# Block operands of the up projection behind the mixer's last tile, adds of squares on GpSimd, and the first up pair's root in a chain of its own

## The chip, the cores and the metric

One core of one Trainium2 chip. The metric is the time of the whole program on the device in microseconds (us). Before the change it was 1103.57 us, the median of three runs (1101.72 to 1104.21). The engines are TensorE (PE in the profile, PEld its weight loads), VectorE (DVE), ScalarE (ACT), GpSimd (POOL) and SyncE (SP). A measurement of this kernel can hardly tell less than 0.2%, some 2.2 us, from no change.

## What is computed

The reference is one layer of a streaming encoder trunk, for a prompt of 512 tokens and a sample of 64, all in float32 with a model width of 1024:

```python
y, c_new, sa, sb = _mixer(_rmsnorm(x, p['norm_mix'][l]), ...)      # gated delta net and gated linear attention
x = x + y
x = x + _cross_attn(_rmsnorm(x, p['norm_mem'][l]), mem_k[l], mem_v[l], p['w_mq'][l], p['w_mo'][l])
f, f_new = _conv_ffn(_rmsnorm(x, p['norm_ffn'][l]), p['w_up'][l], ..., p['w_down'][l], ffn_prev[l])
x = x + f
...
return (_rmsnorm(x, p['norm_final']), ...)

def _rmsnorm(x, g):
    y = x * lax.rsqrt(jnp.mean(x * x, axis=-1, keepdims=True) + EPS)
    return y * g
```

`_conv_ffn` multiplies by `w_up` (1024 to 2 x 2816), runs a causal depthwise convolution of width 3, gates one half with the SiLU of the other and multiplies by `w_down`. `_cross_attn` has four heads of 256 that look into 256 memory tokens. What matters here are the three last norms (`norm_mem`, `norm_ffn` and `norm_final`, called n2, n3 and final below): each needs, for every token, the sum of the squares of x over all 1024 features.

## The kernel before

Both token sets run together as 576 columns, with the features on the partitions: x is eight tiles `x[0]` to `x[7]` of 128 x 576. An up operand has 580 columns, since each token set has two columns of padding. Each product of float32 is made of three products of half-length parts: an operand is split into a high part (`xh`, `ach`, `sh`, written by an ACT cast) and a low one (`xl`, `acl`, `sl`, the difference, written by DVE or POOL), and weights likewise (`w`, where the low part of many of them is finished by a DMA that accumulates in memory, issued from POOL's queue behind an ACT copy). Many products of two tiles by two go through a scheme of seven products on sums of blocks (P1, P2, P3, Q4 to Q7), whose operands are differences such as `tu` and `tw`, split again.

**Order of the work.** The kernel's text does not put instructions in the order in which they run. A class `Driver` records them with a model of each engine's time. The main generator yields PE work in its order. Side work (norms, operands, convolutions) lies in chains that `spawn` starts and that go on when what they have waited for is there: `yield [tiles]` waits for tiles, `yield WAIT` and `yield (key,)` for something in `drv.done`. Each instruction is put on its engine's queue by its modelled start, and `flush` (the line L257 of nearly all rows) issues it. `V`, `A` and `G` are DVE, ACT and POOL; `X` is whichever of DVE and POOL the model says ends sooner. A change in one chain can thus move rows of others.

**Squares.** `sq_acc` (L784) adds the square of one tile to a sum: ACT squares into `sq` (for the first tile into the sum itself), then X adds, `acc <- acc, sq`. It serves n2 (in `c_norm`, while the mixer's last product wo finishes its tiles), n3 (in `c_mo`, sum `facc`) and the final norm (in `last_tile`, in the tail). In the program before, all 19 of these adds went to DVE: 7, 7 and 5. `c_rstat` (L799) then reduces the sum over the partitions with one-column matmuls (`sm<-keep,acc`, ten in the trace for five token blocks), takes the root on POOL (`rt`), makes diagonal matrices `dg` on DVE and spreads them with matmuls (`sm<-dg,onesr`); ACT copies the outcome to `rbc`.

**Between the attention and the up projection.** The product mo of the attention's output adds into x. Tile 0 and tile 1 are plain products, the other six go through the scheme. PE does tile 0, then the three pairs, then tile 1 (`mo_last(1)`, read out of the large PSUM bank by `x<-big,x`). As soon as a tile of x is whole, `c_mo(m)` (L1879) squares it, scales it by the gain of n3 (`cx`), splits it to `xh` and `xl`, and marks `("mo", m)`. When both tiles of a pair are marked it spawns `c_sums(k)` (L1897), which makes the block operands of the up projection: `tu` and `tw` on DVE or POOL, their splits `sh`, `sl`, `sw`. They are used only from the fifth pair of up tiles on; the first four pairs (`JS = 4`) are plain. `first_up` (L1951) is the first up tile: it takes the x tiles in the order 2, 3, 4, 5, 0, 6 and then 7, 1, each as soon as it is marked.

**The first up pair.** An up pair is the tiles j and 22 + j, gate and value. Since the root of n3 is not there when the first pair ends, `raw_evac` copies that pair out of PSUM unscaled. The main loop then waited for "n3", called `use_norm("n3")` and spawned the convolution chains `c_gate` and `c_act` of pair 0, all ahead of the second pair's first tile. Later pairs are scaled by `rbc` when they are read out (`up_evac`).

**The tail.** The last stage is the down product; `last_tile` squares each finished tile of x into `acc` and scales it for the output (`gx`), and the last two tiles are done in halves with their own squares. One-column matmuls sum over the partitions, POOL makes the roots `rtf`, PE transposes, and `yo` rows scale the result.

PSUM has two large banks' tiles (`big`) and four small ones (`sm`): PE can start the next product in a bank only when the readout of the one before has been done.

Of the kernel before, what the change touches and what calls it, by code (L numbers as in the profile page):

```python
# [14 lines left out]
ALU = mybir.AluOpType  # L15
# [137 lines left out]
WAIT = "wait"  # L153
# [305 lines left out]
def tile_trunk(ctx, tc, xT, memT, wt, wd, vec, cst, w0, wgate, st_gdn, st_conv, st_gla, st_ffn, ckT, cv,  # L459
               o_y, o_gdn_p, o_conv, o_gla_p, o_ffn, o_mk, o_mv, o_gdn_s, o_gla_s):  # L460
    nc = tc.nc
    drv = PE = Driver(nc.tensor, nc.sync)
    V, A, G = Engine(drv, "V", nc.vector), Engine(drv, "A", nc.scalar), Engine(drv, "G", nc.gpsimd)
    X = Either(V, G)
# [19 lines left out]
    def slot(s="s", dt=F32, w=SLOT):  # L484
        return drv.rotate("s", NS, sp.tile([P, w], dt, tag="s", name=nm(s)))
# [42 lines left out]
    def r4(ap, b=128):  # L528
        return ap.rearrange("p (a b) -> p a b", b=b)
# [254 lines left out]
    def sq_acc(acc, x_, first, w=T):  # L784
        s = acc if first else slot("sq")
        A.activation(s[:, :w], x_[:, :w], AF.Square)
        if not first:
            X.tensor_tensor(acc[:, :w], acc[:, :w], s[:, :w], op=ALU.add)

    def ssq(accs, t, n, ps):  # L790

# [51 lines left out]
    def use_norm(key):  # L843
        N["rt"], N["rbc"] = N[key]
# [89 lines left out]
    def conv_raw(ps, copy):  # L934
        u = slot("u")
        for o, i in zip(two(u, 3, 518), pv(ps)):
            copy(o, i)
        return u
# [564 lines left out]
    def parts2(h, lo, src):  # L1503
        A.copy(h, src)
        X.tensor_tensor(lo, src, f(h), op=ALU.subtract)
# [8 lines left out]
    def hl2(src, new=None):  # L1514
        h, lo = [(new or slot)(s, F32R) for s in ("ach", "acl")]
        parts2(h[:, 0:T], lo[:, 0:T], src[:, 0:T])
        return h[:, 0:T], lo[:, 0:T]
# [66 lines left out]
    def main():  # L1584
        acc = slot("acc")
# [50 lines left out]
        for k in range(KT + 1):  # L1636
            for i, ps in enumerate(first2):
                j = k - i
# [31 lines left out]
        u0 = conv_raw(b0[0], A.copy)  # L1670
# [98 lines left out]
        def c_gate(g0, g1, r):  # L1769
            yield [g0, g1]  # L1770
            X.tensor_tensor(g1[:, N2], g1[:, N2], r[:, N2], op=ALU.mult)
            X.tensor_tensor(g0[:, 0:T], g0[:, 0:T], r[:, 0:T], op=ALU.mult)
            A.activation(g1[:, 0:T], g1[:, 0:T], AF.Tanh, scale=-0.5)
            A.activation(g0[:, 0:T], g0[:, 0:T], AF.Tanh, scale=0.5)
# [36 lines left out]
        acc = slot("acc")  # L1811
# [84 lines left out]

        def c_sums(k):  # L1897

            (eh, el, ce), (oh_, ol_, co) = fx[2 * k], fx[2 * k + 1]
            yield [ce, co]  # L1900
            u, w = slot("tu"), slot("tw")
            X.tensor_tensor(u[:, U1], ce[:, U1], ce[:, U2], op=ALU.subtract)
            X.tensor_tensor(u[:, U2], co[:, U2], ce[:, U2], op=ALU.subtract)
            yield [u]
            V.scalar_tensor_tensor(w[:, U1], u[:, U2], -1.0, ce[:, U1], op0=ALU.mult, op1=ALU.subtract)
            h, lo = slot("sh", F32R), slot("sl", F32R)
            parts2(h[:, 0:580], lo[:, 0:580], u[:, 0:580])
            yield [w]
            V.scalar_tensor_tensor(w[:, U2], w[:, U1], -1.0, co[:, U1], op0=ALU.mult, op1=ALU.subtract)
            w1 = slot("sw", F32R)  # L1910
            parts2(w1[:, U1], w1[:, U2], w[:, U1])
            sops[k].update({"P1": (eh[:, U1], el[:, U1]), "P2": (oh_[:, U1], ol_[:, U1]), "P3": (oh_[:, U2], ol_[:, U2]),
                            "Q5": (h[:, U1], lo[:, U1]), "Q7": (h[:, U2], lo[:, U2]), "Q6": (w1[:, U1], w1[:, U2]), "Q4": (eh[:, U2], el[:, U2])})
            drv.done.add(("sops", k))
            while not drv.ready("plain"):
                yield WAIT
            parts2(eh[:, U2], el[:, U2], w[:, U2])
            drv.done.add(("sop4", k))
# [51 lines left out]
        def states(col, u):  # L1970
            G.tensor_copy(u[:, 514:516], fst[:, col, :])
            G.tensor_copy(fout[:, col, :].rearrange("p (a b) -> p a b", b=2), pads(u))

        def up_tile():
            u = slot("fu")
            G.memset(u[:, 0:2], 0.0)
            return u

        def up_evac(col, ps):
            u = up_tile()  # L1980
            if isinstance(ps, Pair):
                V.together([("tensor_tensor", (u[:, 2 + c:292 + c], ps[:, i, 0:290], N["rbc"][:, c:c + 290]), dict(op=ALU.mult)) for i, c in ((0, 0), (1, 290))])
            else:
                V.tensor_tensor(r4(u[:, 2:582], 290), ps[:, :, 0:290], r4(N["rbc"][:, 0:580], 290), op=ALU.mult)
            states(col, u)
            return u
# [67 lines left out]
        def c_act(j, u, raw=False):  # L2054
            c1 = yield from up_conv(NJ + j, u, raw)
            while not drv.ready(("gate", j)):
                yield WAIT
            if j == NJ - 1:
                DMO(o_ffn, fout)
            c0 = cs[j]  # L2060
            yield [c0, c1]
            for a, b in ((0, 0), (TP, TP + 2)):
                n = TP if a == 0 else TS
                X.tensor_tensor(c1[:, a:a + n], c0[:, b:b + n], c1[:, b:b + n], op=ALU.mult)
            p = max(q for q in range(4) if PART0[q] <= j)
            odd_ = (j - PART0[p]) % 2
            yield [c1]
            full[j] = hl2(c1)
            cs[j] = c1
            if odd_ and p == 3:  # L2070
                yield from inner(j - 1, j, cs.pop(j - 1), cs.pop(j), True)
            drv.done.add(("act", j))

        full, ops = {}, {}

        def inner(ke, ko, ce, co, whole):
# [20 lines left out]
        acc = slot("acc")  # L2097
        gx = []
        for kd, i in FFN[:-1]:
            if kd == "up":  # L2100
                j = i
                ba_, bb_ = [], []
                if j == 0:
                    ba_.append(wide())
                    yield from first_up(ba_[0])
                    xs = [(fx[k][0][:, 0:580], fx[k][1][:, 0:580]) for k in range(8)]
                else:
                    yield from tile_proj("up", j, xs, ba_, None, 580, wide)
                if j == 0:
                    yield from tile_proj("up", NJ, xs, bb_, None, 580, wide)  # L2110
                    u0, u1 = raw_evac(ba_[0]), raw_evac(bb_[0])
                    yield ("n3",)
                    use_norm("n3")
                    drv.spawn(c_gate(j, u0, True), 1)
                    drv.spawn(c_act(j, u1, True), 1)
                    continue
                drv.spawn(c_gate(j, up_evac(j, ba_[0])), 1)
                if j > 0:
                    yield from tile_proj("up", NJ + j, xs, bb_, None, 580, wide)
                if j == JS - 1:  # L2120
                    drv.done.add("plain")
                drv.spawn(c_act(j, up_evac(NJ + j, bb_[0])), 1)
            elif kd == "upx":
                yield tuple(("sop4" if i[1] == "Q4" else "sops", k) for k in range(4))
                yield from up_product(*i)
            elif kd == "dn1":
                m, p = i
                yield tuple(("act", j) for j in PARTS[p])
                wh, wl = weight("dn", i)
                ps = wide()  # L2130
                yield from proj(ps, wh, wl, act_of(p), late=True)
                V.together([("tensor_tensor", (xx, xx, i_), dict(op=ALU.add)) for i_, xx in pieces(ps, x[m])])
                if m == 7:
                    for k in PARTK[p]:
                        del full[k]
            elif kd == "dns":
                ks = PARTS[i[0][0][1][1]]
                yield tuple(("act", j) for j in ks)
                yield from products(i, [ops[k] for k in ks[0::2]], dn_finish)
            else:  # L2140

                yield tuple(("act", j) for j in PARTS[3][:-1])
                halves = []
                for m in i:
                    ps = big()
                    wh, wl = weight("dn", (m, 3), m == i[0], m != i[0])
                    yield from proj(ps, wh, wl, [full[k] for k in PARTK[3][:-1]], True, False, late=True)
                    halves.append((ps, wh, wl))
                yield (("act", NJ - 1),)
                for m, (ps, wh, wl) in zip(i, halves):  # L2150
                    yield from proj(ps, wh, wl, [full[NJ - 1]], False, True, k0=len(PARTS[3]) - 1)
                    for xx, i_ in zip(two(x[m]), pv(ps)):
                        V.tensor_tensor(xx, xx, i_, op=ALU.add)
                    last_tile(m)
# [277 lines left out]
```

## Time and profile before

| | us |
|---|---|
| median of three runs | 1103.57 |
| the profiled execution | 1103.1 |
| its span, first to last instruction | 1101.2 |
| PE busy | 1084.6 |
| DVE busy | 745.0 |
| ACT busy | 702.8 |
| POOL busy | 313.5 |
| mean granted TensorE clock | 0.997 of full |

PE works in 98% of the span, so the other engines count where PE waits for them. Such waits are listed by who was waited for. A row of the timeline gives the start, the duration, the engine, the operation, the tile written, `<-`, the tiles read, and the shape; neighbours of one kind are drawn together as "x2", and the bracket at a row's end is the idle time ahead of it and what ended that. All names carry no numbers there, so `acc` stands for the sums of all norms.

### The profile page before, as it was taken

What the parts mean: (1) busy time and instruction counts of PE and PEld (TensorE: products, weight loads), DVE (VectorE), ACT (ScalarE), POOL (GpSimd) and SP (SyncE); (2) the same over time, 40 slices, a digit from 0 to 9 for tenths busy, and PEclk for the clock granted to TensorE, in tenths of its full rate; (3) what the DMA queues carried; (4) which work ended last, traced back from release to release, by engine and by line L of the source; (5) the groups of instructions that cost most, each with busy time, mean ns of one, the idle gap of its engine ahead of it and who ended that gap; (6) DMA issues with size and microseconds to landing.
All of it is one profiled execution on the core that took longest, in us unless ns stands there. A gap on an engine that the chain in (4) does not pass through costs nothing. (4 is left out here: it accounts for less than half of the span.)

```text
span 1101.2 us, 21348 instructions
## 1 busy us (share of the span) xinstructions
PE 1084.6 (98%) x8206; PEld 1045.5 (95%) x8206; DVE 745.0 (68%) x1464; ACT 702.8 (64%) x1383; POOL 313.5 (28%) x541
## 2 busy tenths in 40 slices
PE   9999999999999999999999999999999999999997
PEld 8999989998988999999999999999999999999996
DVE  5666854864655866887655768667876677577665
ACT  6766646563755568476655658768866676667644
POOL 1344215230422232022101223234332342333221
PEclk9999999999999999999999999999999999999999
DMA  9666433353445788789683629767886886888844
GB/s 306 142 160 142 98 78 96 61 122 97 137 100 144 176 169 184 277 237 207 165 229 61 189 46 204 182 134 163 175 198 150 184 198 158 191 179 182 171 83 111
DMA packets 66885, 173.04 MB, mean 157 GB/s; under 512 B 7776, under 2 KB 14048, under 8 KB 66784
## 3 DMA queue, kind: packets, MB, share of 16 engines
q0 software_dynamic: 30096, 72.89, 38.7%
q1 hardware_dynamic: 36400, 98.26, 27.3%
q8 instruction: 65, 1.06, 0.4%
q10 hardware_dynamic: 288, 0.52, 0.1%
q14 instruction: 36, 0.29, 0.1%
HBM read 158.67 MB, written 5.37 MB: 149 GB/s over the span
## 5 line engine op out<-in xcount | busy, mean ns | idle before, releaser
L257 PE MATMUL big<-xh,w 128*128 128x256 f32 (+2 forms) x1568 | 290.7, 302 | 1.2 <-ACT xh L257 1.0
L257 PEld LDWEIGHTS big<-xh,w 128*128 128x128 f32 x1568 | 234.2, 189 | 7.0 <-issue 1.5
L257 POOL DMA_DIRECT2D w<-wt x147 | 133.6, 915 | 372.6 <-ACT w L257 314.5
L257 ACT ACTIVATE w<-wr 128x512 fp32r<-128x512 f32 (+3 forms) x180 | 142.9, 795 | 56.1 <-PE sm L257 25.2
L257 ACT CAST w<-wr 128x512 fp32r<-128x512 f32 (+3 forms) x201 | 158.8, 792 | 25.7 <-PE big L257 9.8
L257 PE MATMUL big<-xl,w 128*128 128x256 f32 (+2 forms) x784 | 167.9, 295 | 0.5 <-DVE xl L257 0.5
L257 PE MATMUL sm<-xh,w 128*128 128x290 f32 (+1 forms) x768 | 162.4, 298 | 0.0
L257 PEld LDWEIGHTS big<-xl,w 128*128 128x128 f32 x784 | 130.9, 188 | 1.0 <-DVE xl L257 0.9
L257 PE MATMUL sm<-ach,w 128*128 128x288 f32 (+2 forms) x624 | 127.1, 296 | 4.3 <-DVE x L257 2.4
L257 PEld LDWEIGHTS sm<-xh,w 128*128 128x128 f32 x768 | 126.9, 190 | 0.0
L257 PE MATMUL big<-ach,w 128*128 128x256 f32 x624 | 111.3, 296 | 0.3 <-ACT ach L257 0.3
L257 PEld LDWEIGHTS sm<-ach,w 128*128 128x128 f32 x624 | 101.0, 188 | 5.7 <-ACT gx L257 1.5
L257 PE MATMUL sm<-xl,w 128*128 128x290 f32 (+1 forms) x384 | 103.5, 299 | 0.0
L257 ACT CAST w<-ws 128x512 fp32r<-128x512 f32 (+1 forms) x124 | 73.4, 601 | 40.6 <-DVE ws L257 20.3
L257 PEld LDWEIGHTS big<-ach,w 128*128 128x128 f32 x624 | 94.7, 188 | 0.6 <-ACT ach L257 0.5
L257 PE MATMUL sm<-acl,w 128*128 128x288 f32 (+2 forms) x312 | 83.8, 295 | 0.0
L257 DVE TENSOR_TENSOR w<-ws,w 128x512 fp32r<-128x512 f32 (+1 forms) x91 | 60.3, 672 | 25.2 <-ACT w L257 24.0
L257 DVE SCALAR_TENSOR_TENSOR fc<-fu,vec,fc 128x578 f32<-128x578 f32 x88 | 70.5, 816 | 9.4 <-ACT fc L257 9.3
L257 PEld LDWEIGHTS sm<-xl,w 128*128 128x128 f32 x384 | 72.1, 191 | 0.0
L257 PE MATMUL big<-acl,w 128*128 128x256 f32 (+1 forms) x312 | 67.1, 297 | 0.3 <-DVE acl L257 0.3
L257 PE MATMUL sm<-sh,w 128*128 128x290 f32 x288 | 60.9, 296 | 0.0
L257 PEld LDWEIGHTS sm<-acl,w 128*128 128x128 f32 x312 | 58.2, 188 | 0.0
(396 smaller groups left out, 2211.1 us busy)
## 6 DMA issues: line engine op xcount, KB each, us to landing
wr<-wt SPq DMA_DIRECT2D x134, 512.0 KB, 5.7
w<-wt POOLq DMA_DIRECT2D x60, 512.0 KB, 6.8
w<-wt POOLq DMA_DIRECT2D x87, 256.0 KB, 6.1
wr<-wd SPq DMA_DIRECT2D x24, 384.0 KB, 5.5
w<-wd POOLq DMA_DIRECT2D x24, 384.0 KB, 6.6
w<-ws POOLq DMA_DIRECT2D x29, 256.0 KB, 4.7
x<-xT SPq DMA_DIRECT2D x16, 288.0 KB, 5.8
mem<-memT SPq DMA_DIRECT2D x8, 256.0 KB, 5.0
```

The costliest lines, as they stand in the source:

```text
L257: fn(*args, **kw)
```

## The change

Three edits:

1. `c_sums` waits until all eight tiles are marked `("mo", m)` before it makes block operands of any pair.
2. The add in `sq_acc` is always POOL's (`G` in place of `X`), in all three norms.
3. A new chain `c_first_up` waits for "n3" and then does what the main loop did for the first pair. The main loop waits for "n3" only in the second pair, ahead of the readout of its first tile.

```diff
--- before.py
+++ after.py
@@ -785,7 +785,7 @@
         s = acc if first else slot("sq")
         A.activation(s[:, :w], x_[:, :w], AF.Square)
         if not first:
-            X.tensor_tensor(acc[:, :w], acc[:, :w], s[:, :w], op=ALU.add)
+            G.tensor_tensor(acc[:, :w], acc[:, :w], s[:, :w], op=ALU.add)
 
     def ssq(accs, t, n, ps):
 
@@ -1896,6 +1896,8 @@
 
         def c_sums(k):
 
+            while not drv.ready(*(("mo", m) for m in range(8))):
+                yield WAIT
             (eh, el, ce), (oh_, ol_, co) = fx[2 * k], fx[2 * k + 1]
             yield [ce, co]
             u, w = slot("tu"), slot("tw")
@@ -2071,6 +2073,13 @@
                 yield from inner(j - 1, j, cs.pop(j - 1), cs.pop(j), True)
             drv.done.add(("act", j))
 
+        def c_first_up(u0, u1):
+            while not drv.ready("n3"):
+                yield WAIT
+            use_norm("n3")
+            drv.spawn(c_gate(0, u0, True), 1)
+            drv.spawn(c_act(0, u1, True), 1)
+
         full, ops = {}, {}
 
         def inner(ke, ko, ce, co, whole):
@@ -2109,11 +2118,9 @@
                 if j == 0:
                     yield from tile_proj("up", NJ, xs, bb_, None, 580, wide)
                     u0, u1 = raw_evac(ba_[0]), raw_evac(bb_[0])
-                    yield ("n3",)
-                    use_norm("n3")
-                    drv.spawn(c_gate(j, u0, True), 1)
-                    drv.spawn(c_act(j, u1, True), 1)
+                    drv.spawn(c_first_up(u0, u1))
                     continue
+                yield ("n3",)
                 drv.spawn(c_gate(j, up_evac(j, ba_[0])), 1)
                 if j > 0:
                     yield from tile_proj("up", NJ + j, xs, bb_, None, 580, wide)
```

**DVE at the end of the mo products.** The names are those of above with a number for each buffer: x_5763, x_5764 and x_5758 are x[6], x[7] and x[1]; acc_7741 is the sum of n3. Before:

```order
L257 TENSOR_TENSOR x_5764<-x_5764,sm_8249 128x288
L257 TENSOR_TENSOR sw_8368<-tw_8248,sw_8368 128x290
L257 SCALAR_TENSOR_TENSOR tw_8404<-tu_8403,cx_8284 128x290
L257 TENSOR_TENSOR sl_8431<-tu_8403,sh_8430 128x580
L257 TENSOR_TENSOR acc_7741<-acc_7741,sq_8432 128x576
L257 SCALAR_TENSOR_TENSOR tw_8404<-tw_8404,cx_8344 128x290
L257 TENSOR_TENSOR xl_8434<-cx_8435,xh_8433 128x580
L257 TENSOR_TENSOR acc_7741<-acc_7741,sq_8445 128x576
L257 TENSOR_TENSOR x_5758<-big_7840,x_5758 128x512
L257 TENSOR_TENSOR x_5758<-big_7840,x_5758 128x64
L257 TENSOR_TENSOR xl_8447<-cx_8448,xh_8446 128x580
L257 TENSOR_TENSOR sw_8464<-tw_8404,sw_8464 128x290
```

And now, from the same readout of x[7] on:

```order
L257 TENSOR_TENSOR x_5764<-x_5764,sm_8244 128x288
L257 TENSOR_TENSOR x_5758<-big_7842,x_5758 128x512
L257 TENSOR_TENSOR x_5758<-big_7842,x_5758 128x64
L257 TENSOR_TENSOR xl_8419<-cx_8420,xh_8418 128x580
L257 TENSOR_TENSOR xl_8431<-cx_8432,xh_8430 128x580
L257 TENSOR_TENSOR xl_8459<-cx_8460,xh_8458 128x580
L257 TENSOR_TENSOR tu_8461<-cx_8184,cx_8113 128x290
L257 TENSOR_TENSOR tu_8463<-cx_8251 128x290
L257 TENSOR_TENSOR tu_8463<-cx_8335,cx_8251 128x290
L257 TENSOR_TENSOR tu_8478<-cx_8420 128x290
```

The adds to the sum and the block operands' rows (`sw`, `sl`, `tw`) have left the stretch ahead of x[1]'s readout (`x_5758<-big`), which now follows the readout of x[7] directly. The block operands' `tu` rows stand behind the three `xl` rows.

**POOL at the same place.** The last adds to n3's sum, between the issues of the weights' DMAs, as they are now:

```order
L257 DMA w_8306<-wt 128x1024
L257 MEMSET cx_8460 128x2x2
L257 DMA w_8355<-wt 128x1024
L257 TENSOR_TENSOR acc_7744<-acc_7744,sq_8417 128x576
L257 TENSOR_TENSOR acc_7744<-acc_7744,sq_8429 128x576
L257 MEMSET rin_8540 128x8
L257 TENSOR_TENSOR acc_7744<-acc_7744,sq_8457 128x576
L257 DMA w_8553<-wt 128x1024
L257 MEMSET fu_8625 128x2
L257 MEMSET fu_8626 128x2
L257 TENSOR_TENSOR rt_8528<-rin_8540,mhalf 128x5
L257 DMA w_8556<-wt 128x1024
```

Before, POOL had here three `tu` rows and a `sw` row of the block operands, and no adds.

**DVE in the tail.** x_5761 and x_5762 are x[4] and x[5], acc_8449 and acc_8433 the final sum. Before:

```order
L257 TENSOR_TENSOR w_13223<-wr_13222,w_13223 128x512
L257 TENSOR_TENSOR x_5760<-x_5760,sm_13146 128x288
L257 TENSOR_TENSOR acc_8449<-acc_8449,sq_13251 128x576
L257 TENSOR_TENSOR acc_8449<-acc_8449,sq_13253 128x576
L257 TENSOR_TENSOR x_5761<-x_5761,sm_13212 128x288
L257 TENSOR_TENSOR x_5761<-x_5761,sm_13224 128x288
L257 TENSOR_TENSOR x_5762<-x_5762,sm_13212 128x288
L257 TENSOR_TENSOR x_5761<-x_5761,sm_13313 128x288
L257 TENSOR_TENSOR x_5762<-x_5762,sm_13212 128x288
L257 TENSOR_TENSOR acc_8449<-acc_8449,sq_13329 128x576
```

And now:

```order
L257 TENSOR_TENSOR w_13223<-wr_13222,w_13223 128x512
L257 TENSOR_TENSOR x_5760<-x_5760,sm_13146 128x288
L257 TENSOR_TENSOR x_5761<-x_5761,sm_13212 128x288
L257 TENSOR_TENSOR x_5761<-x_5761,sm_13224 128x288
L257 TENSOR_TENSOR x_5762<-x_5762,sm_13212 128x288
L257 TENSOR_TENSOR x_5761<-x_5761,sm_13292 128x288
L257 TENSOR_TENSOR x_5762<-x_5762,sm_13212 128x288
```

The three adds of 128 x 576 have left this queue; the readouts follow one another.

**PE at the last attention head.** `sm<-kvh,qh`, `kvl,qh` and `kvh,ql` are the scores of the last head, where the number of the second `qh` (before 7739, now 7742) is that of the head's last query tile; `big<-ach,w` and `big<-acl,w` are mo's first plain product. Before:

```order
L257 MATMUL sm_7721<-pth_7553,kvh_6733 128x512
L257 MATMUL sm_7721<-ptl_7554,kvh_6733 128x512
L257 MATMUL sm_7721<-pth_7553,kvl_6734 128x512
L257 MATMUL sm_7722<-pst_7559,cvr_7116 128x64
L257 MATMUL sm_7744<-kvh_7501,qh_7618 128x256
L257 MATMUL sm_7744<-kvl_7502,qh_7618 128x256
L257 MATMUL sm_7744<-kvh_7501,ql_7619 128x256
L257 MATMUL sm_7744<-kvh_7501,qh_7739 128x256
L257 MATMUL sm_7744<-kvl_7502,qh_7739 128x256
```

And now:

```order
L257 MATMUL big_7753<-ach_7236,w_7431 128x256
L257 MATMUL big_7753<-ach_7236,w_7431 128x320
L257 MATMUL big_7753<-acl_7237,w_7431 128x256
L257 MATMUL big_7753<-acl_7237,w_7431 128x320
L257 MATMUL big_7753<-ach_7236,w_7432 128x256
L257 MATMUL big_7753<-ach_7236,w_7432 128x320
L257 MATMUL sm_7789<-kvh_7505,qh_7621 128x256
L257 MATMUL sm_7789<-kvl_7506,qh_7621 128x256
L257 MATMUL sm_7789<-kvh_7505,ql_7622 128x256
L257 MATMUL sm_7789<-kvh_7505,qh_7742 128x256
L257 MATMUL sm_7789<-kvl_7506,qh_7742 128x256
L257 MATMUL sm_7789<-kvh_7505,ql_7743 128x256
```

Twelve mo matmuls, of which the last six are shown, now stand ahead of the scores. Before, the scores followed the preceding head's products with the values directly. Further on, n3's `sm<-dg,onesr` stand some 40 matmuls further down, in the first tile of the second up pair in place of the second tile of the first; behind that PE's order is as it was.

## The prediction

> **What bounds the kernel now.** I read the page first, then the waits of TensorE, then the chain of waits, and last the timeline around the three gaps that the change can reach.
>
> ```profile
> span 1101.2 us, 21348 instructions
> PE 1084.6 (98%) x8206; PEld 1045.5 (95%) x8206; DVE 745.0 (68%) x1464; ACT 702.8 (64%) x1383; POOL 313.5 (28%) x541
> ```
>
> PE (TensorE) is busy for 1084.6 of 1101.2 us. The change leaves every matmul in the program, so only the 16.6 us in which PE does not work, and stretches in which it works slowly, can be won. The profiled execution took 1103.1 us, 1.9 more than its span; it lies 0.47 under the median of the runs shown (1103.57, from 1101.72 to 1104.21).
>
> ```profile
> PE sm L257 <- DVE x L257: 2.4, 3, 1.3
> PE big L257 <- ACT xh L257: 1.0, 1, 1.0
> PE sm L257 <- ACT qh L257: 0.8, 1, 0.8
> PE big L257 <- DVE xl L257: 0.5, 2, 0.3
> PE sm L257 <- DVE ql L257: 0.3, 1, 0.3
> ```
>
> These rows give us in total, times, longest. The `xh` and `xl` waits stand between the attention's output products (tile family `mo`) and the up projection; one `x` wait of 1.3 stands in the tail; `qh` and `ql` stand ahead of the last head's scores. The other waits I leave as they are.
>
> **The gap between mo and up.** The timeline, with start, duration, engine and tiles:
>
> ```profile
> 683.68 1.04 ACT L257 CAST w<-wr 128x1024 fp32r<-128x1024 f32 x1
> ...
> 685.53 0.68 ACT L257 ACTIVATE sq<-x 128x576 f32<-128x576 f32 x1
> ...
> 686.37 0.43 PE L257 MATMUL big<-ach,w 128*128 128x256 f32 x2
> ...
> 687.03 0.75 DVE L257 TENSOR_TENSOR acc<-acc,sq 128x576 f32<-128x576 f32 x1
> ...
> 687.74 0.68 ACT L257 ACTIVATE sq<-x 128x576 f32<-128x576 f32 x1
> ...
> 689.92 0.81 DVE L257 TENSOR_TENSOR x<-big,x 128x512 f32<-128x512 f32 x2
> ...
> 690.82 0.69 ACT L257 ACTIVATE sq<-x 128x576 f32<-128x576 f32 x1 [0.46 <-DVE x L257]
> ...
> 692.44 0.68 ACT L257 CAST xh<-cx 128x580 fp32r<-128x580 f32 x1
> ...
> ...
> 693.17 0.54 PE L257 MATMUL big<-xh,w 128*128 128x290 f32 x2 [0.97 <-ACT xh L257]
> ...
> 693.96 0.54 PE L257 MATMUL big<-xl,w 128*128 128x290 f32 x2 [0.26 <-DVE xl L257]
> ...
> 694.34 1.16 PE L257 MATMUL sm<-keep,acc 128*128 128x1 f32 x10
> ```
>
> PE ended tile 1's product at 686.80, but DVE read it out only at 689.92, behind sums of squares and rows of the block operands, and ACT worked on operand casts meanwhile. So `xh` of tile 1 came at 693.12, and PE, free at 692.20 (693.17 less 0.97), waited 0.97 and then 0.26 for `xl`.
>
> In the changed order the readout follows the last readout of tile 7 directly and starts at about 686.9. ACT then sets the pace. With no operand casts, its square of tile 6 starts when the weight cast ends, 683.68 + 1.04 = 684.72. From square to square a tile takes 687.74 - 685.53 = 2.21, so tile 7 starts at 686.93 and tile 1 at 689.14. From tile 1's square to its `xh` are 692.44 - 690.82 = 1.62: `xh` runs 690.76 to 691.44, and `xl` follows to 692.20. PE wants `xh` at 692.20 and `xl` about 0.27 later. **Both waits go: 0.97 + 0.26 = 1.23 us**, with margins of 0.76 and 0.27.
>
> **The slow stretch behind it.** The windows (PE busy, ..., then the granted clock):
>
> ```profile
> 693.10:695.50 2.40, 2.08 (x15) 1.81 (x15) 2.40 (x5) 2.40 (x5) 1.14 (x1) 1.00 0.00 0
> 695.97:699.38 3.41, 3.41 (x16) 3.41 (x16) 2.28 (x9) 3.41 (x4) 3.17 (x4) 0.50 0.62 159
> 1086.40:1087.80 1.40, 1.40 (x15) 1.33 (x13) 1.13 (x5) 0.79 (x3) 0.00 (x0) 1.00 0.00 0
> ```
>
> Right behind these waits the clock stood at 0.50 for 3.41 us, in which PE does half of its work: 1.71 us lost. What preceded it is two gaps and ten one-column matmuls of 1.16 us in all. The tail's one-column matmuls at 1086.4, without a gap among them, kept 1.00, and the 1.33 gap at 1079.01, without such matmuls, is followed by no drop either (the mean clock of the run, 0.997, has room only for this stretch and one after PE's last work). So I take both to be needed, and without the gaps **1.71 us come back**. Bounds: 0, if the ten matmuls suffice, and 1.71.
>
> [...]
>
> **The squares on GpSimd.** No `acc` add ran on POOL before. The nearest row of its size, and the row of the adds on DVE:
>
> ```profile
> L257 POOL TENSOR_TENSOR acl<-ao,ach 128x576 fp32r<-128x576 f32 x2 | 2.8, 1424 | 21.6 <-ACT ach L257 21.6
> ...
> L257 DVE TENSOR_TENSOR acc<-acc,sq 128x576 f32<-128x576 f32 x26 | 19.6, 753 | 0.7
> ```
>
> So 19 adds leave DVE (19 x 0.753 = 14.3 us of its time, mostly in PE's shadow) and cost POOL 1.42 each, or 1.75 as in the row of 375.03 below, which has company on DVE; I take 1.42 where nothing collides. For `norm_ffn` the last three adds follow the squares that end at 685.4, 687.6 and 689.8: they end at 686.9, 689.1 and 691.3 (with 1.75, 691.6). PE reaches the ten matmuls that read the sum at about 692.20 + 2 x 0.27 = 692.75. Margin 1.2 us, so no wait. POOL's DMA for the next weights stands behind the last add, but it waits for ACT's cast of about 691.4 to 692.5 anyway.
>
> Where both engines run at once:
>
> ```profile
> 375.03 1.75 POOL L257 TENSOR_TENSOR acl<-tu,ach 128x576 fp32r<-128x576 f32 x1
> 375.10 2.30 DVE L257 TENSOR_TENSOR gt<-gt,gt 128x576 f32<-128x576 f32 x1
> ```
>
> A DVE row with two operands in SBUF, which alone takes 0.75 (the `acc` row has its shape), took 2.30: 1.55 longer. Each of the 19 adds can do this to a DVE row that makes an operand or stands ahead of a readout. In the two product stages (wo and mo, 7 adds each) DVE has rows of both sorts, but it is idle about a third of the time (68% busy), and PE has four banks of the small sort to go on with, so I expect few that reach PE. **I book 0.6 us of new waits; the bounds are 0 and, if all 14 of these adds passed on 1.55 less the 0.75 that each saves, 11 us.** [...]
>
> **The tail.**
>
> ```profile
> 1076.88 1.61 DVE L257 TENSOR_TENSOR acc<-acc,sq 128x576 f32<-128x576 f32 x2
> ...
> 1078.41 1.01 DVE L257 TENSOR_TENSOR x<-x,sm 128x288 f32<-128x288 f32 x2
> 1079.01 0.37 PE L257 MATMUL sm<-ach,w 128*128 128x288 f32 x1 [1.33 <-DVE x L257]
> ...
> 1082.63 0.67 ACT L257 ACTIVATE sq<-x 128x576 f32<-128x576 f32 x1
> ...
> 1085.41 0.48 DVE L257 TENSOR_TENSOR acc<-acc,sq 128x320 f32<-128x320 f32 x1
> ...
> 1086.48 0.28 PE L257 MATMUL sm<-keep,acc 128*128 128x1 f32 x2
> ```
>
> Two adds stood on DVE ahead of the readout that frees PE's bank. Without them it starts at about 1077.0 and ends at 1077.45, before PE wants the bank (1079.01 - 1.33 = 1077.68). **The gap goes: 1.33 us**, and all behind it moves up. POOL's last add then follows a square that ends at 1083.30 - 1.33 = 1081.97; the one before it ends at 1082.15, so the last ends at 1083.6 (with 1.75 each, 1084.2). DVE wants it for the add of 320 columns at 1085.41 - 1.33 = 1084.08. It just fits (or is 0.1 late), and PE wants the sum only at 1085.15. Bounds: 0 (POOL sets the end) and 1.33.
>
> **The order in the attention.** The moved n2 rows also shift the planner's choices: 12 mo matmuls now stand ahead of the last head's scores.
>
> ```profile
> 627.72 0.39 PE L257 MATMUL sm<-kvh,qh 128*128 128x256 f32 x1 [0.79 <-ACT qh L257]
> ...
> 632.22 0.28 PE L257 MATMUL sm<-kvh,ql 128*64 128x256 f32 x1
> ...
> 632.87 0.70 PE L257 MATMUL big<-ach,w 128*128 128x256 f32 x4
> ...
> 635.96 0.35 DVE L257 TENSOR_SCALAR e<-e,sc 64x256 f32<-64x256 f32 x1
> ```
>
> Four such matmuls took 0.70 and two (686.37, above) 0.43, so one more is 0.135. The twelve, 1.6 us, cover the 0.79 and the 0.3 for `ql`; `ach` is now cast ahead of `qh`, which costs 0.7 of that cover, so about 0.3 of the waits stays. **0.8 us gained**; bounds 0 and 1.09. The softmax behind the scores keeps 36 mo matmuls (4.9 us) as cover; from the last scores (632.50) to the last `e` (636.31) it took 3.8.
>
> **The first up pair's root.** Its `sm<-dg,onesr` matmuls go some 40 matmuls down, and with them the normalised readouts and convolutions of pair 0. The second pair's readout waits for the same root:
>
> ```profile
> 703.50 0.95 PE L257 MATMUL sm<-dg,onesr 128*128 128x512 f32 x4
> ...
> 711.67 0.76 DVE L257 TENSOR_TENSOR fu<-big,rbc 128x580 f32<-128x580 f32 x1 [0.88 <-PE big L257]
> ...
> 745.41 0.30 PE L257 MATMUL sm<-sh,w 128*128 128x290 f32 x1
> ```
>
> The readout begins when PE ends the tile. With the root's matmuls 40 x 0.135 = 5.4 later, at about 709, their 0.95 us and the copies of `rbc` behind them (some 0.7, as other ACT rows of 512 and more columns here) end near 710.6, so this costs PE nothing; a bank freed a us late is asked for again only a whole up tile later. The block operands are now made after 691.4; PE first reads them at 745.41, 54 us later. Nothing.
>
> **The sum.** 1.23 + 1.71 + 1.33 + 0.8 - 0.6 = 4.5 us: 1103.1 - 4.5 = 1098.6 by the profiled execution, 1099.1 by the median. I say 1099.0.
>
> **The rivals.**
>
> *The gate falls all the same* (0.20). The ten matmuls suffice, or some other short wait joins them: 4.5 - 1.71 = 2.8 us, 1100.3 to 1100.8. For it: they are there still. Against it: the tail's like stretch.
>
> *Late weights* (0.14). Adds wait for their squares with DMA issues behind them on POOL, and PE waits for weights as it did in this row:
>
> ```profile
> 664.72 0.93 PE L257 MATMUL sm<-ach,w 128*128 128x288 f32 x5 [0.93 <-DMA w<-wt]
> ```
>
> Two or three issues late by 1.42 cost 2.8 to 4.3 and take the gain back: 1101.5 to 1103. Against it: the adds stand between issues that wait for ACT casts for us on end.
>
> *The held port* (0.13), on the other side. In the wo and mo products the adds hold up DVE's weight sums and `xl` rows, the readouts queue behind them, and PE waits for banks. Each that reaches PE costs 1.55 - 0.75 = 0.8. It decides from (4.5 + 2.2) / 0.8, some 8 of the 14 adds: 1106 and more.
>
> *It does not do what it says*: POOL's chain of adds becomes the tail's end, 1.33 less gain, 1100. This lies in the forecast's range.
>
> **How the numbers follow.** The forecast, 1097 to 1101, has 0.53; with the three rivals that is 1.00. The low end of 1097.0 is the whole sum without new waits (5.1) and some 1 us of bank and weight waits in the mo products that may move; the high end of 1103.8 takes in late weights. Left out: the held port and some slivers. A measurement here can tell about 0.2%, 2.2 us, from no change: faster is under 1101.4. Faster 0.66 (0.50 of the forecast, 0.15 of the first rival, 0.01 of the second), same 0.20 (0.03, 0.05, 0.12), slower 0.14 (0.01 of late weights, and the port).
>
> **What would show it.** Right: no PE wait on `xh` and `xl` near 692; no clock of 0.5 before PE's last work; no 1.33 wait in the tail; `acc` rows on POOL of about 1.42; `sm<-keep,acc` near 691 with no wait ahead. Wrong: PE waits on POOL's `acc`; DVE rows of 2 us beside POOL's adds with PE waiting on `x`; longer waits on `w<-wt`.

## The result, and the profile after

The changed kernel takes **1098.71 us**, median of ten runs (1098.12 to 1101.05), against 1104.12 (1101.09 to 1106.91, ten runs) before: a ratio of **0.9954**, 95% interval 0.994 to 0.9968, so 5.1 us less by the ratio. The profiled execution took 1098.48 us. In a second comparison (experiment e10) the ratio was 0.9964 (0.9948 to 0.9979). The forecast was 1099.0, and the sum made against the profiled execution 1098.6.

The head of the page and the waits of PE (in total, times, longest) in the changed kernel:

```profile
span 1096.7 us, 21365 instructions
PE 1082.6 (99%) x8206; PEld 1043.8 (95%) x8206; DVE 736.6 (67%) x1449; ACT 703.5 (64%) x1383; POOL 342.7 (31%) x556
```

```profile
PE sm L257 <- ACT fu L257: 1.2, 2, 0.9
...
PE sm L257 <- DVE x L257: 0.8, 2, 0.6
PE sm L257 <- DMA w<-wt: 0.8, 1, 0.8
...
PE big L257 <- ACT w L257: 0.6, 1, 0.6
PE big L257 <- ACT ach L257: 0.5, 1, 0.5
PE sm L257 <- ACT w L257: 0.4, 1, 0.4
...
PE sm L257 <- DVE ql L257: 0.3, 1, 0.3
...
PE big L257 <- DVE xl L257: 0.2, 1, 0.2
```

Of the `fu` row, the kernel before had:

```profile
PE sm L257 <- ACT fu L257: 0.7, 1, 0.7
```

PE is busy for 2.0 us less with the same 8206 matmuls, which shows that it worked faster somewhere, and the span is 4.5 shorter. The `xh` and `qh` rows of before are gone, the `x` row has lost its wait of 1.3, and a second wait on `fu` and two on `w` are new. The `w` wait of 0.6 stands at 6.39, far ahead of the change's places; e1 and e11 have one of 0.8 there as well.

Between mo and up the timeline now reads:

```profile
685.30 0.82 DVE L257 TENSOR_TENSOR x<-big,x 128x512 f32<-128x512 f32 x2 [1.14 <-PE big L257]
...
685.63 1.44 POOL L257 TENSOR_TENSOR acc<-acc,sq 128x576 f32<-128x576 f32 x1 [0.76 <-ACT sq L257]
...
686.04 2.32 DVE L257 TENSOR_TENSOR xl<-cx,xh 128x580 fp32r<-128x580 f32 x2
...
687.84 1.81 POOL L257 TENSOR_TENSOR acc<-acc,sq 128x576 f32<-128x576 f32 x1 [0.73 <-ACT sq L257]
...
688.63 0.68 ACT L257 CAST xh<-cx 128x580 fp32r<-128x580 f32 x1
...
689.35 0.92 DVE L257 TENSOR_TENSOR xl<-cx,xh 128x580 fp32r<-128x580 f32 x1 [0.99 <-ACT xh L257]
...
690.65 0.43 PE L257 MATMUL big<-xh,w 128*128 128x290 f32 x2
...
691.20 0.28 PE L257 MATMUL sm<-keep,acc 128*128 128x1 f32 x2
```

The readout of tile 1 now waits for PE (1.14), not PE for it. `xh` ends at 689.31, and PE takes it up at 690.65 without a wait, and `xl` ends at 690.27. The last add on POOL ends at 689.65, 1.55 us ahead of the one-column matmuls. The clock, by windows (the granted clock stands behind POOL's column):

```profile
680.00:692.40 12.40, 12.40 (x95) 12.24 (x94) 8.52 (x16) 11.44 (x19) 6.86 (x10) 1.00 0.76 176
692.40:700.00 7.60, 7.60 (x57) 7.60 (x58) 5.80 (x16) 7.40 (x13) 5.25 (x4) 1.00 0.90 245
```

The 0.50 is gone and PE has no idle time in 20 us.

**Where the time came from.** Of single matmuls that are the same in both profiles, the starts:

| matmul | before | after | gained so far |
|---|---|---|---|
| `big<-xh,w`, ahead of the last head | 621.41 | 621.32 | 0.09 |
| `big<-ach,w`, behind its scores | 633.68 | 632.48 | 1.20 |
| `big<-xh,w`, first up tile | 691.50 | 690.11 | 1.39 |
| `big<-xh,w`, second up pair | 711.48 | 706.87 | 4.61 |
| `sm<-ach,w`, ahead of the tail's gap | 1077.39 | 1074.42 | 2.97 |
| `sm<-ach,w`, behind it | 1079.01 | 1074.57 | 4.44 |
| the last one | 1094.60 | 1090.06 | 4.54 |

The attention brought 1.1, the passage from mo to up 3.2, the tail 1.5; between the second up pair and the tail 1.6 were given back.

### The profile page after: what moved, and what is told of

It is laid out like the page before. It is cut to its first block, busy times and chain, and to the rows that moved or that the text cites. A ratio compares the mean times of both kernels' runs of the same rounds, so it can differ in the third digit from the quotient of the medians.

```text
span 1096.7 us, 21365 instructions
## 1 busy us (share of the span) xinstructions
PE 1082.6 (99%) x8206; PEld 1043.8 (95%) x8206; DVE 736.6 (67%) x1449; ACT 703.5 (64%) x1383; POOL 342.7 (31%) x556
## 4 chain that ended last, share of the span: by engine, by line
PE 90%; DMA 3%; ACT 2%; issue 2%; DVE 2%; POOL 1%; SPq 0%; DVEq 0%; ACTq 0%; POOLq 0%
PE sm L257 45%; PE big L257 45%; DMA w<-ws 2%; ACT w L257 1%; DMA w<-wt 1%; DVE ws L257 0%; DMA wr<-wt 0%; DVE fc L257 0%; POOL w L257 0%; ACT ach L257 0%; POOL ws L257 0%; ACT vraw L257 0%; DVE x L257 0%; DVE acl L257 0%; ACT fc L257 0%
```

## The experiments

Twelve kernels ran, in three groups of four, each group on one chip with runs of the kernel before: e1 to e4 and e9 to e12 on one chip, e5 to e8 on another. Ratios are against that kernel in the same group. The changed kernel itself did not run beside e5 to e8, so where these are set against it, its two ratios (0.9954 and 0.9964) are used. For the clock I count executions with a mean of 0.997 or less; of the kernel before, 52 of the 90 beside these experiments were such, and in the first group their median was 2.1 us above that of the others (1104.07 and 1101.93).

**e1, the first edit alone**

```diff
         def c_sums(k):
 
+            while not drv.ready(*(("mo", m) for m in range(8))):
+                yield WAIT
```

> The kernel before with the first edit alone: block operands wait for all eight tiles; adds stay where they were, the root stays in the main loop. My theory: what delayed tile 1 between mo and up was the work on block operands (DVE rows and ACT casts), and one add of 0.75 ahead of the readout can be borne, since x[7]'s readout ends at 685.7 and the readout could start at 686.85. So both waits (1.23) and the slow stretch (1.71) go: 2.9 to 3.2 us faster than before, the tail's wait of 1.3 and the attention's 1.1 stay. Rival: it was the adds on DVE that delayed tile 1; then the waits stay for the larger part and the gain is under 1 us.

Measured: 0.9983 (0.9973 to 0.9992), 1.9 us faster. Of this kernel:

```profile
686.37 0.82 DVE L257 TENSOR_TENSOR x<-big,x 128x512 f32<-128x512 f32 x2
...
689.69 0.68 ACT L257 CAST xh<-cx 128x580 fp32r<-128x580 f32 x1
...
691.27 0.75 DVE L257 TENSOR_TENSOR xl<-cx,xh 128x580 fp32r<-128x580 f32 x1
```

The readout came 3.5 us earlier than before, PE's wait on `xh` was gone, that on `xl` 0.07, and the clock stayed at 1.00: this edit alone clears the passage, and the adds on DVE were not its cause. The gain is smaller than the 2.9 to 3.2 expected. The slow stretch is not in each execution of the kernel before: 3 of 12 executions had the low clock here, 18 of 33 there, so what goes with it is an estimated 0.3 x 2.1 = 0.6 us in the median, not 1.71; with the 1.23 that makes the 1.9.

**e2, the second edit alone**

```diff
-            X.tensor_tensor(acc[:, :w], acc[:, :w], s[:, :w], op=ALU.add)
+            G.tensor_tensor(acc[:, :w], acc[:, :w], s[:, :w], op=ALU.add)
```

> The kernel before with the second edit alone: all adds of squares on POOL. My theory: the tail's wait goes (1.3 us) and the attention's waits on qh and ql shrink by about 1.1; between mo and up ACT still makes the block operands' casts and DVE reads tile 1 out behind sl, sw, sl rows, so xh comes late still and the clock falls: 2.4 us faster, at most 3.5. Rival: the adds were the cause there as well, then 5 to 6 us faster (all of the change's gain).

Measured: 0.9972 (0.9961 to 0.9984), 3.1 us faster, between the 2.4 and the 3.5 expected. The passage from mo to up in this kernel:

```profile
685.04 1.61 POOL L257 TENSOR_TENSOR acc<-acc,sq 128x576 f32<-128x576 f32 x1 [1.89 <-ACT sq L257]
685.28 1.99 DVE L257 TENSOR_TENSOR sl<-tu,sh 128x580 fp32r<-128x580 f32 x1
...
687.58 1.42 POOL L257 TENSOR_TENSOR acc<-acc,sq 128x576 f32<-128x576 f32 x1 [0.93 <-ACT sq L257]
687.93 1.69 DVE L257 TENSOR_TENSOR xl<-cx,xh 128x580 fp32r<-128x580 f32 x1
...
689.78 1.50 POOL L257 TENSOR_TENSOR acc<-acc,sq 128x576 f32<-128x576 f32 x1 [0.78 <-ACT sq L257]
689.91 1.68 DVE L257 TENSOR_TENSOR sw<-tw,sw 128x290 fp32r<-128x290 f32 x1
```

```profile
689.67 0.54 PE L257 MATMUL big<-xl,w 128*128 128x290 f32 x2 [1.28 <-DVE xl L257]
...
692.32 0.54 PE L257 MATMUL big<-xl,w 128*128 128x290 f32 x2 [0.22 <-DVE xl L257]
```

A DVE row beside each add on POOL took longer: `sl` 1.99 and `sw` 1.68, in the kernel before 0.76 and 0.45, and `xl` 1.69, there 0.75. Two `xl` rows come late and PE waits 1.28 and 0.22. The theory was wrong in two points: the wait on `xh` is gone, and the clock mostly held (1.00 through this passage, low in 2 of 10 executions), although the two waits together are longer than the 1.23 of before. The longer one now ends 2.4 us before the other begins, and so farther from the one-column matmuls. Here the longer rows reach PE; with the first edit the `sl` and `sw` rows are elsewhere, and they do not.

**e3, the third edit alone** (the new chain `c_first_up`, and the wait for "n3" in the second pair, as in the diff of the change)

> The kernel before with the third edit alone: the first up pair's root in a chain. My theory: the root is on no path that PE waits for, since no gap stood at the second tile's end: no change within 0.3 us. Rival: the later root frees the order behind it, 0.5 us or more faster.

Measured: 1.0002 (0.9993 to 1.0011), no change. The three single edits make 1.9 + 3.1 - 0.2 = 4.8 us, and the whole 4.0 to 5.1. Both e1 and e2 have fewer executions with the low clock, so this share of the gain is in that sum twice.

**e4, only the final norm's adds on POOL**

```diff
-    def sq_acc(acc, x_, first, w=T):
+    def sq_acc(acc, x_, first, w=T, E=None):
...
-            X.tensor_tensor(acc[:, :w], acc[:, :w], s[:, :w], op=ALU.add)
+            (E or X).tensor_tensor(acc[:, :w], acc[:, :w], s[:, :w], op=ALU.add)
...
-            sq_acc(acc, x[m], m == 0)
+            sq_acc(acc, x[m], m == 0, E=G)
```

> The kernel before with only the five adds of the final norm on POOL. My theory: the PE wait of 1.33 in the tail goes and all behind it moves up, 1.3 us faster, with no other row moved. Rival: POOL's chain of adds at 1.42 each takes over as what ends last in the tail; then 0 to 0.5.

Measured: 0.9989 (0.9979 to 0.9999), 1.2 us faster, and its profile has no wait in the tail: against before, PE's matmuls gain 1.34 us across the place of that wait, so POOL's chain does not take over. It is the profile that rules the rival out. The time alone would not, since only 3 of 12 executions had the low clock, though the slow stretch ahead of the tail is still in the profile, and among the others the medians are only 0.4 us apart (1101.51 here, 1101.93 before).

**e5, xh late again**

```diff
-            A.together([("activation", (c_[:, a], x[m][:, b], AF.Identity), dict(scale=g))
-                        for a, b in ((slice(0, TP), slice(0, TP)), (slice(TP + 2, TP + 2 + TS), slice(TP, T)))])
+            scale = [("activation", (c_[:, a], x[m][:, b], AF.Identity), dict(scale=g))
+                     for a, b in ((slice(0, TP), slice(0, TP)), (slice(TP + 2, TP + 2 + TS), slice(TP, T)))]
+            again = scale[:1] * 4 if m == 1 else []
+            A.together(scale + again, extra=-A.weigh(again)[0])
```

> The changed kernel with four repeats of tile 1's scaling row (128x512) on ACT ahead of its xh cast, which the planner doesn't count, so that no other instruction moves. About 2.4 us more on ACT brings back the wait on xh, some 1.1 us, and 0.25 on xl, right ahead of the ten one-column matmuls. My theory (short waits and one-column matmuls close together lower the clock, where the window falls so): 1.3 us of waits, and in about half of the executions a mean clock of 0.997 or less as before the change (18 of 33), the others 0.998 or 0.999; the median 1.5 to 3 us above the changed kernel. Rival (the clock has nothing to do with this place): 1.3 us above, and the clock at 0.998 or 0.999 in nine of ten executions, as in the changed kernel.

Measured: 1.0001 (0.9988 to 1.0013), so the whole gain is gone, and 11 of 12 executions had the low clock. In the profile PE waited 0.83 on `xh`, 0.27 on `xl`, and ahead of them 0.50 on weights. The repeats did not cause the 0.50: the weights' DMA had been issued at 679.78 and ACT began tile 1's scaling at 687.91. Then:

```profile
691.78:695.20 3.42, 2.38 (x17) 2.12 (x18) 2.67 (x7) 3.07 (x5) 1.03 (x3) 1.00 0.04 10
695.20:698.61 3.41, 3.41 (x17) 3.41 (x16) 3.27 (x9) 3.41 (x4) 2.44 (x1) 0.50 1.01 173
```

The clock does hang on this place: e8, on the same chip and without the waits, had the low clock in 2 of 10. The loss, 4 to 5 us against the changed kernel, is more than the 1.5 to 3 expected; five executions had a mean clock of 0.994 to 0.996, which would be more than one slow window, but only the profiled one (0.997) shows its windows.

**e6, the same, with the one-column matmuls later**

```diff
             while not drv.ready(*(("mo", m) for m in range(8))):
                 yield WAIT
+            yield 10.0
             drv.spawn(c_rstat("n3", [(facc, 0)], 4, True, 2.0, None, TP + 2))
...
                 yield ("n3",)
+                while j == 1 and drv.step() is True:
+                    pass
```

> The same late xh, but the ten one-column matmuls (and the root behind them) follow some 34 matmuls further down, 4.6 us later. My theory: the wait alone doesn't lower the clock: 1.3 us above the changed kernel, clock 0.998 or 0.999 in nine of ten executions. Rival (the wait alone is enough): as the run before, with 0.997 in about half of the executions.

Measured: 0.9986 (0.9975 to 0.9996), and 6 of 11 executions with the low clock. Between the two theories: the waits alone (1.59 and 0.26 in the profile, which has no slow window) seem to do it, less often. Where the slow windows of the six lay is not shown; e7 and e12 settle that one-column matmuls are not needed, so "both to be needed" was wrong.

**e7, POOL late**

```diff
-            G.tensor_tensor(acc[:, :w], acc[:, :w], s[:, :w], op=ALU.add)
+            calls = [("tensor_tensor", (acc[:, :w], acc[:, :w], s[:, :w]), dict(op=op)) for op in (ALU.add, ALU.subtract, ALU.add)]
+            G.together(calls[:1 + again], extra=-G.weigh(calls[1:1 + again])[0])
...
-            sq_acc(facc, x[m], m == 0)
+            sq_acc(facc, x[m], m == 0, again=2 * (m == 1))
```

> The changed kernel with the last add of n3's sum done three times on POOL (added, subtracted, added), unseen by the planner. The add then ends 2.9 us later, at about 692.5 where PE is at the one-column matmuls at 691.2. My theory: a wait of 1.3 us right ahead of the ten matmuls, so 1.3 us and the slow window in about half of the executions: 1.5 to 3 us above the changed kernel. This is the price of POOL being late, and it says how much room the adds had there: 1.5 us. Rival: PE doesn't wait for the sum or waits little (under 0.5 us), since something else sets the time of the matmuls.

Measured: 0.9994 (0.998 to 1.0007), 3.3 to 4.4 us above the changed kernel, more than the 1.5 to 3 expected; 7 of 12 with the low clock. PE waited 1.99 us for POOL:

```profile
PE sm L257 <- DMA w<-wt: 2.7, 1, 2.7
PE sm L257 <- POOL acc L257: 2.0, 1, 2.0
```

So the room that the adds have is real and about 1 to 1.5 us wide. The slow window of this profile came elsewhere, behind the 2.7 us on weights:

```profile
662.27:665.68 3.41, 0.70 (x6) 0.46 (x4) 0.80 (x2) 0.53 (x2) 0.89 (x1) 1.00 1.07 278
665.68:669.10 3.42, 3.41 (x14) 3.41 (x15) 1.06 (x2) 2.04 (x4) 0.89 (x2) 0.50 0.28 60
692.99:696.40 3.41, 1.69 (x13) 1.45 (x11) 3.41 (x3) 1.45 (x2) 3.25 (x3) 1.00 0.12 34
696.40:699.81 3.41, 3.14 (x24) 3.11 (x25) 3.41 (x10) 2.48 (x3) 1.99 (x5) 1.00 0.49 73
```

A window in which PE was busy for 0.70 of 3.41 us is followed by half clock, and one with 1.69 is not. Nor is the next, with 0.27 us of wait and 1.26 of one-column matmuls.

**e8, the adds of n2 back on DVE** (as e4, with `E=G` at the calls of n3 and of the final norm, and the first and third edits)

> The changed kernel with the seven adds of n2 given back to the choice of the planner (DVE); n3's and the final norm's adds stay on POOL, the other edits too. My theory: the attention's order goes back, with PE's waits on qh and ql of 0.8 and 0.3: 1.1 us slower than the changed kernel, still 3.5 to 4 us faster than before. [...]

Measured: 0.997 (0.9956 to 0.9984), 0.7 to 1.8 us above the changed kernel by its two ratios, as expected but within the error. In the profile the waits of 0.79 on `qh` and 0.29 on `ql` are back.

**e9, tile 0's split later, and e10, the changed kernel again.** PE waited 0.8 to 2.7 us for weights at 663 to 667 in every profile so far; e9 puts work that is not urgent behind ACT's casts for them.

```diff
         def c_mo(m):
             yield [x[m]]
+            if m == 0:
+                yield 4.0
```

> The changed kernel with the scaling and splitting of mo's tile 0 (cx, xh, xl) put behind the next casts of weights on ACT: c_mo(0) waits four modelled us. It isn't wanted before the first up tile, and the weights' DMAs can be issued some 1.6 us earlier. PE's order is unchanged. In the runs so far PE waited 0.8 to 2.7 us for a w<-wt at 663 to 666. My theory: that wait falls by up to 1.6 us, so 0.8 to 2 us faster than the changed kernel on the same chip, and fewer executions with a slow window. Rival: the DMA, not its issue, sets the time (its data come late for other traffic), and the wait stays within 0.5 us of what it was.

> The changed kernel itself, on the same chip as the run before: 0.9954 of the time before the change, within 0.002, the clock at 0.998 or more in most executions. If its gain were mostly luck of the chip that it first ran on, it would be under 2 us here.

Measured: e9 0.9965 (0.9953 to 0.9977), e10 0.9964 (0.9948 to 0.9979), the same, so the expected 0.8 to 2 us did not come. Of e9, and then of e10:

```profile
PE sm L257 <- DMA w<-ws: 2.8, 3, 1.5
...
PE sm L257 <- DMA w<-wt: 0.4, 1, 0.4
```

```profile
PE sm L257 <- DMA w<-wt: 1.4, 1, 1.4
...
PE sm L257 <- DMA w<-ws: 1.0, 2, 0.6
```

The wait on `w<-wt` fell by 1.0, as meant, and a wait on later weights (`w<-ws`) of 0.93 at 674 took its place. The other 1.9 us of e9's `w<-ws` stand at 490 and 500, ahead of the edit's place. The gain of the change holds on this chip, and all six executions kept the high clock.

**e11, the kernel before with the one-column matmuls later** (the third edit, and the lines of e6 with 8.0 in place of 10.0)

> The kernel before with the third edit (which alone changed nothing) and the ten one-column matmuls of n3 some 38 rows later on PE. The waits on xh and xl (1.23 us) stay. Theory: the clock halves for a window of 3.41 us when about half of a window (1.5 to 1.8 us) is waits and one-column matmuls together; the waits alone are 1.23 and don't reach that, the two together do, where the window falls so. Then the share of executions at 0.997 or less falls from over half to under a quarter, and the median is 0.8 to 2 us faster than before. Rival (the waits alone do it, or something else in the run): the share and the median as before.

Measured: 1.0003 (0.999 to 1.0017), and 3 of 11 executions with the low clock against 11 of 24 of the kernel before on that chip. The profile has both waits (0.97 and 0.27) and no slow window behind them. The share fell as expected, though so few executions prove little; the median did not fall by the expected 0.8 to 2 us. Part of the price is seen: the later root raised a wait on `fu` at 749.55 from 0.75 to 1.42.

**e12, one long wait** (e6 with nine repeats)

> The changed kernel with nine repeats of tile 1's scaling row and with the one-column matmuls later: one wait of about 4.4 us on xh, with no one-column matmuls near. Any window grid has over 2 us of it in one window. Theory as in the run before: the clock halves in nearly all executions (0.997 or less in nine of ten), 4.4 + 1.7 = 6 us or a little more above the changed kernel. Rival (one-column matmuls are needed for it): the clock at 0.998 or more in most executions, and 4.4 us above.

Measured: 1.0028 (1.0017 to 1.0038), 7.5 us above e10's median, and 10 of 11 executions with the low clock.

```profile
693.16:696.58 3.42, 0.54 (x5) 0.31 (x3) 0.00 (x0) 3.29 (x5) 0.00 (x0) 1.00 0.00 0
696.58:699.99 3.41, 0.93 (x3) 0.64 (x3) 0.95 (x2) 3.26 (x6) 0.00 (x0) 0.50 0.00 0
699.99:703.40 3.41, 3.41 (x14) 3.41 (x15) 3.41 (x10) 3.41 (x4) 1.74 (x2) 0.50 0.43 58
703.40:706.80 3.40, 3.40 (x28) 3.40 (x27) 2.35 (x6) 3.40 (x6) 1.05 (x4) 1.00 1.02 277
```

The wait was 5.36 us, and two windows at half clock followed, the first of which still held the wait's end (PE busy for 0.93). One-column matmuls are not needed for it.

## Why the prediction was right

- **mo to up, 1.23 us: right, with more room than forecast.** The matmuls ahead of it had gained 1.39 us (table). With these added, tile 1's `xh` ran at 690.02 to 690.70 in the time of before (forecast 690.76 to 691.44) and PE came at 692.04 (forecast 692.20). ACT's squares follow one another by 2.2 us, as forecast; the whole row of them is 0.7 earlier because the weight cast ahead ended at 683.75 in the time of before (forecast 684.72). e1 and e2 show whose work it was: the first edit's.
- **The slow stretch, 1.71 us: the place right, the size and the reason not.** In the two profiles it came back whole: the passage gained 3.2 against 2.94. But over executions it is a matter of chance: the low clock, wherever it lay, came 52 times in 90 before and once in 16 after (the ten runs of the result and the six of e10). At 2.1 us apiece that is an estimated 1.1 us in the mean; that the profiled execution of before had the stretch was luck. And "both to be needed", of the gap and the ten matmuls, fell with e7 and e12. What the traces show is when the clock changed. In the kernel before it first rose 6.48 us into the span, fell 202 times 3.413 us after that (695.97), rose 3.413 us later (699.38) and fell again 320 times 3.413 us after the first rise (1098.74). In the changed kernel it rose at 5.38 and fell 319 times 3.413 us later (1094.24). The table counts windows of 3.413 us from the first rise of each execution, which came between 4.05 us (e11) and 7.08 us (e12) into the span. One-column time is counted from the end of the product ahead:

| kernel, window from | waits | one-column | clock of the next |
|---|---|---|---|
| e12, 693.16 | 2.88 | 0 | 0.5 |
| e7, 662.27 | 2.72 | 0 | 0.5 |
| e5, 691.78 | 1.03 | 0.99 | 0.5 |
| before, 692.56 | 0.87 | 0.99 | 0.5 |
| e7, 692.99 | 1.72 | 0 | 1.0 |
| e3, 691.92 | 1.23 | 0.47 | 0.5 |
| e4, 661.94 | 1.58 | 0 | 1.0 |
| e4, 692.66 | 1.23 | 0.24 | 0.5 |
| e2, 660.78 | 1.56 | 0 | 1.0 |
| e7, 696.40 | 0.27 | 1.26 | 1.0 |
| e11, 1092.90 (PE's work ends in it) | 1.91 | 0 | 1.0 |
| e4, 1095.42 (PE's work ends in it) | 2.61 | 0 | 0.5 |

  The row of e11, and the window behind it, in which the clock still stands at 1.00:

```profile
1092.90:1096.31 3.41, 1.50 (x14) 1.26 (x12) 2.06 (x3) 1.73 (x3) 0.00 (x0) 1.00 0.77 236
1096.31:1099.72 3.41, 0.00 (x0) 0.00 (x0) 0.00 (x0) 0.00 (x0) 0.00 (x0) 1.00 0.89 302
```

  In the profiles of the kernel before and of the changed one no other window up to PE's last work had more than 0.93 us of the two together, and full clock followed each. In the table idle time alone was followed by full clock at 1.56 (e2), 1.58 (e4), 1.72 (e7) and 1.91 (e11), and by half clock at 2.61 (e4), 2.72 (e7) and 2.88 (e12). With one-column matmuls half clock followed four sums of 1.47 to 2.02 (e4, e3, before, e5), and full clock the 1.53 of e7, so the sum of the two alone does not tell which follows, and the "1.5 to 1.8 us" of e11's theory is not shown as a threshold. Why e3's and e4's slow stretches lasted two windows stays open; in both, part of the ten one-column matmuls (0.80 and 1.23 us) ran in the first slow window, and in before and e5, with one slow window, none did.
- **The tail, 1.33 us: right.** 1.5 came (table), and in e4's profile 1.34. POOL's last add ended at 1080.71, and DVE's add of 320 columns followed at 1080.94, ahead of the matmuls at 1082.04:

```profile
1077.77 2.95 POOL L257 TENSOR_TENSOR acc<-acc,sq 128x576 f32<-128x576 f32 x2 [1.28 <-ACT sq L257]
...
1080.94 0.48 DVE L257 TENSOR_TENSOR acc<-acc,sq 128x320 f32<-128x320 f32 x1
...
1082.04 0.28 PE L257 MATMUL sm<-keep,acc 128*128 128x1 f32 x2
```

- **The attention, 0.8 us: right.** One wait of 0.26 on `ql` is left of the 1.09, as forecast, and by the starts of the matmuls 1.1 came; e8 has both waits back.

```profile
628.89 0.38 PE L257 MATMUL sm<-kvh,ql 128*128 128x256 f32 x1 [0.26 <-DVE ql L257]
```

- **New waits, 0.6 us: too small, and in another place.** They were booked for the wo and mo products. There the wait on `ach` grew from 0.26 to 0.48 and no other did. Instead 1.6 us went in the up product, which the prediction had put at nothing. Of the changed kernel, and then of the kernel before:

```profile
745.11 1.88 PE L257 MATMUL sm<-sw,w 128*128 128x290 f32 x12 [0.90 <-ACT fu L257]
...
784.37 0.40 PE L257 MATMUL sm<-sh,w 128*128 128x290 f32 x1 [0.28 <-ACT fu L257]
...
873.28 0.37 PE L257 MATMUL sm<-xh,w 128*128 128x290 f32 x1 [0.42 <-ACT w L257]
```

```profile
749.55 1.88 PE L257 MATMUL sm<-sw,w 128*128 128x290 f32 x12 [0.75 <-ACT fu L257]
```

  e10 has these waits with 0.89, 0.27 and 0.13, so the `fu` waits belong to the change. None of the single edits has the one at 784, and e1 has neither on `fu`; what brings them stays open. By the starts of the same matmuls around them, the three places took back 0.17, 0.55 and 0.67 us of the 1.6; the rest I can't place.
- **The price of an add on POOL, 1.42: too small, without harm.** The 19 took 1.64 on average, the longest 2.51:

```profile
L257 POOL TENSOR_TENSOR acc<-acc,sq 128x576 f32<-128x576 f32 x19 | 31.2, 1640 | 17.3 <-ACT sq L257 17.2
```

  DVE's rows took longer beside them, as the rival said (`xl` twice in 2.32 above, 0.75 each alone; `w<-ws` 2.02 at 517.12, 0.69 in the median), but no wait of PE hung on it. In e2 two did: whether the longer rows cost time depends on what DVE has to do beside the adds.
- **The first pair's root, nothing: right by itself** (e3).
- **The rivals.** The clock did not fall all the same: it stood at 1.00 through the passage and was low in 1 of 16 executions. Late weights did not take the gain: the wait on `w<-wt` was 0.81 (0.93 before) and 1.39 in e10, and the gain stood in both. Beside POOL's adds DVE's rows took longer, but none that PE waited for; no run shows the port that this rival is named after, only such times of rows.

The errors cancelled, so how near the number came is partly luck: the three gains made 5.8 us where 5.1 had been added up, and 1.6 in place of 0.6 were given back; the table's remaining 0.3 lie in the mo products and at the ends.

## What to carry to other kernels

When PE is at 98%, add up the waits that a change removes and look at the granted clock behind each: here waits of 1.10 (e5) to 1.23 us (before) with one-column matmuls close by were followed by a clock of 0.50 for 3.41 us or twice that, in some executions and not in others (2.1 us between the medians), so judge them by many runs. Moving work to a slower engine (here 1.64 us an add on POOL, 0.75 on DVE) pays when that engine has time of its own before its result is wanted; here it had 1.5 us, and 2.9 more (e7) took back nearly the whole gain. Where rows of the two engines take longer beside each other (`sw` 1.68 in place of 0.45 in e2), first move the less urgent rows out of the same stretch: here the first edit did that for the second.

## What the runs showed of the hardware

- Windows of 3.41 us in which PE stood for 2.61 (e4), 2.72 (e7) and 2.88 us (e12) were followed by a clock of 0.50, and those with 1.56 (e2), 1.58 (e4), 1.72 (e7) and 1.91 (e11) and no one-column matmuls by full clock. With one-column matmuls in the window 0.50 followed four sums of both, from 1.47 (e4) to 2.02 us (e5), and full clock followed 1.53 (e7). The clock first rose 6.48 us into the span in the kernel before, 5.38 in the changed one, 4.05 in e11 and 7.08 in e12.
- The wait on weights near 664 ranged from 0.8 to 2.7 us over thirteen profiles (all but e9's). The runs of the kernel before beside e1 to e4 lie between 1100.48 and 1105.43; that the clock and these waits make this spread is likely, but only the clock was counted over its runs.
- An add of 128 x 576 on POOL and a DVE row with two operands in SBUF took longer beside each other, now the one and now the other: POOL's add took 2.51 beside a DVE row of 128 x 1024 (1.43 at 1073.50, beside readouts alone), and in e2 DVE's `sw` took 1.68 in place of 0.45 beside POOL's add. Readouts with one operand in PSUM (`x<-x,sm`, 128 x 288) kept their 0.45 beside such adds in the changed kernel.
